# A two-layer hybrid encoder on one core: in the FFN's second product, low parts issued with their high parts and one of them moved to VectorE, and the last residual kept in quarters

## The chip, the cores and the metric

The kernel runs on 1 core of one Trainium2 chip. The metric is the time on the device of one execution, in microseconds; of three executions of the kernel before the median is 2655.85 us (2652.89 to 2661.12). Differences of about 0.3% (8 us) are what a measurement of this kernel can tell from none. All numbers of the trace come from one profiled execution, which took 2654.51 us.

## The reference

Two pre-norm residual layers on a sequence of 1024 tokens with 1024 channels, all in float32: a gated DeltaNet layer, then a chunked softmax attention layer, each followed by a gated feed-forward network with a short causal convolution, and a final RMSNorm.

```python
def conv_ffn(xn, w_up, conv_w, conv_b, w_down):
    h = causal_dwconv(xn @ w_up, conv_w) + conv_b
    gate, val = h[..., :FFN_DIM], h[..., FFN_DIM:]
    return (jax.nn.silu(gate) * val) @ w_down

def reference(x, ...):
    h = x
    for layer in range(2):
        h = h + (gated_deltanet(...) if layer == 0 else chunk_attention(...))
        h = h + conv_ffn(rmsnorm(h, f_norm[layer]), f_w_up[layer], f_conv[layer], f_conv_b[layer], f_w_down[layer])
    return rmsnorm(h, final_norm)
```

FFN_DIM is 2816, that is 22 blocks of 128 channels for the gate and 22 for the value.

## The kernel before, in words

**High and low parts.** A float32 operand of a matrix product is cut in two: a high part, a rounded copy that ScalarE (ACT) makes (`cut_high`, line 1378), and a low part, the difference of the operand and its high part (`cut_low`, through the helper of line 1357), which GpSimd (POOL) or VectorE (DVE) computes. `triple` (lines 1390 to 1392) then issues three matmuls for each product: high by high, low by high, high by low. TensorE (PE) so needs both parts, and a low part that is late stops it at the second or third matmul.

**The FFN.** Both layers call `ffn`. The first product (`w_up`) is made per block j of 128 channels, and both products are made by a scheme of seven block products in place of eight, with sums and differences of the operands made before and of the results after. A product of the first kind is `product(j, n)`: its operand `uh`, `ul` is cut from the weights `r` by `operand`, one step of VectorE where a difference is needed (`r<-r,r`), one of ScalarE, one of GpSimd. Results go to `keep`, `gpre` and `vpre` (`after`), then through the three taps of the convolution (`taps`: `val` and `gate`, lines 1473 and 1476), `silu` (line 1479) and `gated` (`val<-val,gate`).

The second product (`w_dn`) takes 18 of the 22 blocks in 9 groups g of two, again with seven block products n, in the order 1, 2, 5, 3, 6, 7, 4 (`ORDER`). One is `second(g, n)`, 12 matmuls into `pd`. Its two operands are `dh`, `dl`, cut from the weights `a` and their sum `ay` by `weights(g, n)`, and `eh`, `el`, cut from the hidden blocks `val` by `channels(g, n)`. `channels` makes the difference that some n need on VectorE (5, 6, 7 and 4), casts `eh` on ScalarE and returns the computation of `el` as a function that is called one step later: on GpSimd for n = 5, 6, 7, on VectorE for 1, 2, 3, 4. The results are copied by ScalarE or added by VectorE into `stage` (`drain`), and GpSimd's queue adds them into DRAM with accumulating DMAs (`send`, line 1711). The last 4 blocks (18 to 21) are multiplied plainly, with weights `fr` loaded by `load_last` and cut to `fh`, `fl` by `cut_last`.

**What sets the order.** The order is written out by hand. `step` appends a piece of work for TensorE to `seq`; `at(i, f, rank)` puts the work of the other engines ahead of step i, by rank within the step. At the end the lists are issued step by step; every engine then runs its own instructions strictly in that order, and waits for data by semaphores. A step of TensorE is 12 matmuls. A second product at step p has `channels` at p - 3 with rank 1.1, the low part at p - 2 with rank 1.1, `weights` at p - 3 with rank 1.2; `operand` has rank 1, `drain` 0, `send` 0.5, taps 2 and more, loads of weights 3. In the steady part a group takes 21 steps: 14 of the first product and 7 of the second, every third one. `eh`, `el`, `dh` and `dl` have two buffers each, `uh` and `ul` three.

**The end of the second layer.** `fin_at` is the step of the last second product, `end` that of the last first product. The residual of the second layer lies in DRAM in `d_r1`, 8 tiles of 128 x 1024 (`quarter` picks 512 columns of one), and `load_r(t)` brings the 128 tokens of tile t from it: for each of two halves c two DMAs of 128 x 2 x 128 each, on SyncE's (SP) queue. TensorE adds them by a transposing matmul (`pf<-ident,res`, line 1863). `load_last(q)` loads the eight pieces of the last weights, also on SP's queue, from `pos[FP - 1, 1]` on, the step of the first product of block 21; `cut_last(q)` follows at `last_at[q]`. SP's queue issues in order. With line numbers of the profile: `a` loads 1652, `d_e` 1715, `fr` 1755 and 1760, `ht` 1836, `res` 1849.

Of the kernel before, what the change touches and what calls it, by code (L numbers as in the profile page):

```python
# [9 lines left out]
F32 = mybir.dt.float32  # L10
# [6 lines left out]
P = 128  # L17
SEQ = 1024
# [4 lines left out]
FP = 22  # L23
# [5 lines left out]
def trunk_kernel(  # L29
# [15 lines left out]
    nc = tc.nc  # L45
# [5 lines left out]
    dram = ctx.enter_context(tc.tile_pool(name="dram", bufs=1, space=bass.MemoryType.DRAM))  # L51
# [72 lines left out]
    def hs(s):  # L124
        return slice(s * HALF, (s + 1) * HALF)
# [370 lines left out]

    ctx_h = ExitStack()

    d_r0, d_r1 = [{(c, s, u): dram.tile([P, SEQ], F32, name=f"d_r{i}_{c}{s}{u}") for c in range(2) for s in range(2) for u in range(2)} for i in range(2)]
    quarter = lambda d, m, s: d[m // 4, s, m % 4 // 2][:, hs(m % 2)]  # L500
    d_y = [[dram.tile([P, HALF], F32, name=f"d_y{k}_{s}") for s in range(2)] for k in range(KT)]
    d_z = [[dram.tile([P, HALF], F32, name=f"d_z{k}_{s}") for s in range(2)] for k in range(KT)]
    d_v = [[dram.tile([P, HALF], F32, name=f"d_v{k}_{s}") for s in range(2)] for k in range(KT)]
# [1 line left out]
    with ExitStack() as ph:  # L505
# [140 lines left out]
        def heads(t):  # L646

            return t // 2, range(4 * (t % 2), 4 * (t % 2) + 4)
# [651 lines left out]
        with tc.manual_schedule(engines={mybir.EngineType.PE, mybir.EngineType.DVE, mybir.EngineType.Activation}):  # L1300
            tails = []
            acts, normed = [[[[None, None] for _ in range(KT)] for _ in range(2)] for _ in range(2)]
            for t in range(4):
                s, hds = heads(t)
# [47 lines left out]
    def ffn(layer, h, hp, xs, tail, d_r, last):  # L1352
# [3 lines left out]
        sub, add = ALU.subtract, ALU.add  # L1356
        tt = lambda eng, o, a, b, op: eng.tensor_tensor(o, a, b, op=op)  # L1357

        d_c = d_r if layer == 0 else {x_: dram.tile([P, SEQ], F32, name=f"d_c{x_[0]}{x_[1]}{x_[2]}") for x_ in d_r}
        d_e = [dram.tile([P, SEQ], F32, name=f"d_e{layer}_{u}") for u in range(2)]  # L1360
        left, right = ExitStack(), ExitStack()
        tp = left.enter_context(tc.tile_pool(name=f"ft{layer}", bufs=1, **SB))
# [9 lines left out]
        def at(i, f, rank=1):  # L1372

            jobs.setdefault(max(i, 0), []).append((rank, f))

        def cut_high(src, ring, copy=nc.scalar.copy):
            hi, lo = [(wd if ring == "e" else wf).tile([P, HALF], F32R, name=ring + x, tag=ring + x, bufs=RINGS[ring]) for x in "hl"]
            copy(hi, src)  # L1378
            return hi, lo

        def cut_low(src, hi, lo, eng):
            tt(eng, lo, src, hi.bitcast(F32), sub)

        def cut(src, ring, copy=nc.scalar.copy):
            hi, lo = cut_high(src, ring, copy)
            cut_low(src, hi, lo, nc.gpsimd)
            return hi, lo
# [6 lines left out]
        kc = [slice(k * P, (k + 1) * P) for k in range(4)]  # L1394
# [129 lines left out]
        pos = {}  # L1524
# [42 lines left out]
        end, fin_at = pos[FP - 1, 7], pos["d", NG - 1, 4]  # L1567
        early = pos["p", 1, 3]
        for i, (j, n) in due.items():
            if i < early:  # L1570
                low = []
# [76 lines left out]
        araw, aops, bops, banks, stage = {}, {}, {}, {}, {}  # L1648

        def load_a(g, q):  # L1650
            araw[g, q] = wd.tile([P, HALF], F32, name=f"a{q}", tag=f"a{q}", bufs=1)
            nc.sync.dma_start(out=araw[g, q], in_=w_dn[(2 * g + q % 10 - 1) * P : (2 * g + q % 10) * P, hs(q // 10 - 1)])

        def weights(g, n):
            a = lambda q: araw[g, q]
            if n == 5:
                araw[g, 0] = wd.tile([P, HALF], F32, name="ay", tag="ay", bufs=1)
                tt(nc.vector, a(0), a(21), a(22), add)
            elif n == 3:
                tt(nc.vector, a(0), a(0), a(11), sub)  # L1660
                tt(nc.vector, a(12), a(12), a(0), sub)
            elif n == 7:
                tt(nc.vector, a(21), a(11), a(21), sub)
            aops[g, n] = cut(a({1: 11, 2: 12, 5: 0, 3: 12, 6: 0, 7: 21, 4: 22}[n]), "d")

        def channels(g, n):
            b11, b12, b21, b22 = [conv_t[2 * g + k, 1][:, hs(s)] for k in range(2) for s in range(2)]
            if n == 5:
                tt(nc.vector, b11, b12, b11, sub)
            elif n == 6:  # L1670
                tt(nc.vector, b11, b22, b11, sub)
            elif n == 7:
                tt(nc.vector, b12, b22, b12, sub)
            elif n == 4:
                tt(nc.vector, b21, b21, b11, sub)
            src = {1: b11, 2: b21, 5: b11, 3: b22, 6: b11, 7: b12, 4: b21}[n]
            bops[g, n] = cut_high(src, "e")
            return lambda: cut_low(src, *bops[g, n], nc.gpsimd if n in (5, 6, 7) else nc.vector)

        def second(g, n):  # L1680
            new = n in (1, 5, 6)
# [38 lines left out]
        for g in range(NG):  # L1720
            p_ = {n: pos["d", g, n] for n in ORDER}
            b_ = {n: pos["d", g - 1, n] for n in ORDER} if g else {1: p_[1] - 4, 3: p_[1] - 4, 7: p_[1] - 4, 4: p_[1] - 3}
            for q, n in ((11, 7), (12, 3), (21, 7), (22, 4)):
                at(b_[n] - 2, lambda g=g, q=q: load_a(g, q), 3 + q / 100)
            for n in ORDER:
                at(p_[n] - 3, lambda g=g, n=n: weights(g, n), 1.2)
                low = []
                at(p_[n] - 3, lambda g=g, n=n, low=low: low.append(channels(g, n)), 1.1)
                at(p_[n] - 2, lambda low=low: low[0](), 1.1)
                at(p_[n] + 1, lambda g=g, n=n: drain(g, n), 0)  # L1730
                if n not in (3, 5):
                    at(p_[n] + 2, lambda g=g, n=n: send(g, n), 0.5)
# [17 lines left out]
        def load_last(q):  # L1750
            tag = ("a11", "a12", "r11", "r21", "r22", "r11", "r22", "r21")[q]
            wp_, bufs = (wd, 1) if tag[0] == "a" else (wf, 2)
            if layer == 0:
                t_ = wp_.tile([P, 4, P], F32, name="fr", tag=tag, bufs=bufs)
                nc.sync.dma_start(out=t_, in_=w_dn[k0 * P :, q * P : (q + 1) * P].rearrange("(k p) m -> p k m", p=P))
                t_ = t_.rearrange("p k m -> p (k m)")
            else:
                k, c = q // 2, q % 2
                t_ = wp_.tile([P, HALF], F32, name="fr", tag=tag, bufs=bufs)
                nc.sync.dma_start(out=t_, in_=w_dn[(k0 + k) * P : (k0 + k + 1) * P, hs(c)])  # L1760
            fw[q] = t_
# [7 lines left out]

        for q in range(8):  # L1770
            s = (1, 1, 2, 3, 4, 4, 5, 6)[q]
            at(pos[FP - 1, s], lambda q=q: load_last(q), 1)
            at(last_at[q], lambda q=q: cut_last(q), 1.5)

        if layer == 0:
# [55 lines left out]
        else:  # L1831
# [8 lines left out]
            def load_r(t):  # L1840

                for c in range(2):
                    if t < 4:
                        tag = ("eh", "el", "dh", "dl")[t % 2 * 2 + c]
                        r_ = (wd if tag[0] == "e" else wf).tile([P, 4, P], F32, name="res", tag=tag, bufs=2)
                    else:
                        r_ = actp.tile([P, 4, P], F32, name="res", tag=f"x{'hl'[c]}{t}_1")
                    for u in range(2):
                        nc.sync.dma_start(out=r_[:, 2 * u : 2 * u + 2], in_=d_r[c, t // 4, u].rearrange("p (f t) -> p f t", f=2)[:, :, kc[t % 4]])
                    res[t, c] = r_  # L1850

            def tile_of(t, ks):
# [358 lines left out]
    def norm_out(t, ht, fin):  # L2211
# [26 lines left out]
        return go()  # L2238

    ctx_f, _ = ffn(1, h, hp, normed, tails[0], d_r1, norm_out)  # L2240
    ctx_f.close()
    ctx_h.close()
# [56 lines left out]
```

## Time and profile before

| | |
|---|---|
| median of three executions | 2655.85 us (2652.89 to 2661.12) |
| the profiled execution | 2654.51 us |
| its span, first to last instruction | 2652.8 us, granted clock 0.994 |
| DVE, ACT, POOL busy | 1907.7, 1409.5, 1483.6 us |
| moved by DMA | 326.72 MB |
| steady second products of layer 0 and 1 | from about 755 to 1283 us and 2029 to 2554 us |
| last blocks and closing of layer 1 | from about 2554 us on |

A row of the timeline has the start, the duration (of several merged instructions, with their count behind the x), the engine, the source line, the operation, the tiles written and read, their shapes, and in brackets how long the engine was idle before and what ended that. L1357 and L1378 are lines of helpers that many operations share; the tiles tell them apart. `PEld` is the weight load of TensorE, which runs beside the matmuls.

### The profile page before, as it was taken

To read this page: it belongs to the slowest core of one execution; us is meant where nothing else is said; L and a number is where in the kernel's file an instruction comes from. 1 tells how busy PE (TensorE), PEld (TensorE's weight loads), DVE (VectorE), ACT (ScalarE), POOL (GpSimd) and SP (SyncE) were. 2 spreads that over 40 slices of the span, in tenths; PEclk is the share of its full clock that TensorE was granted. 3 is DMA by queue.
4 is the path that set the end of the run, shared out by engine and by line. 5 is a ranking of instruction groups with operands and counts; after the bars stand their busy time and mean duration, and the time that the engine had idled before them with its cause. 6 is when DMAs were issued, how large, how long until landed. Compare 5 with 4: busy or idle time off the path is not lost. (4 is left out here: it accounts for less than half of the span.)

```text
span 2652.8 us, 39417 instructions
## 1 busy us (share of the span) xinstructions
PE 2533.4 (95%) x13933; PEld 2067.2 (78%) x13933; DVE 1907.7 (72%) x3084; ACT 1409.5 (53%) x2714; POOL 1483.6 (56%) x1490
## 2 busy tenths in 40 slices
PE   7999899999999999999999999998999999999988
PEld 5878788888777777777778888887777777777767
DVE  5755764553788888888775666666478888888876
ACT  5444456564455555555455555555345555555543
POOL 3655544346367777777645444443344677777760
PEclk9999999999999999999999999999999999999999
DMA  4534435555337777667731111114232577776785
GB/s 127 139 99 119 121 105 156 157 163 165 88 89 154 146 149 143 136 142 155 195 113 48 51 51 48 43 48 141 91 93 84 142 140 147 146 149 139 150 183 175
DMA packets 317846, 326.72 MB, mean 123 GB/s; under 512 B 33232, under 2 KB 240848, under 8 KB 317648
## 3 DMA queue, kind: packets, MB, share of 16 engines
q1 hardware_dynamic: 286192, 219.07, 28.2%
q0 software_dynamic: 26560, 96.48, 20.9%
q10 hardware_dynamic: 4896, 8.65, 0.9%
q8 instruction: 110, 1.80, 0.3%
q14 instruction: 88, 0.72, 0.1%
HBM read 180.94 MB, written 143.20 MB: 122 GB/s over the span
## 5 line engine op out<-in xcount | busy, mean ns | idle before, releaser
L1357 POOL TENSOR_TENSOR ul<-r,uh 128x512 fp32r<-128x512 f32 x282 | 442.9, 1579 | 360.9 <-ACT uh L1378 348.1
L120 PE MATMUL acc<-xh,whi 128*128 128x512 f32 x896 | 375.1, 419 | 0.2 <-ACT xh L1096 0.2
L1378 ACT CAST uh<-r 128x512 fp32r<-128x512 f32 x296 | 180.0, 621 | 365.7 <-DVE r L1357 308.6
L121 PE MATMUL acc<-xl,whi 128*128 128x512 f32 x896 | 353.6, 395 | 1.6 <-POOL xl L379 1.0
L122 PE MATMUL acc<-xh,wlo 128*128 128x512 f32 x896 | 353.1, 394 | 0.5 <-POOL wlo L105 0.5
L105 POOL TENSOR_TENSOR wlo<-wraw,whi 128x256 fp32r<-128x256 f32 (+1 forms) x293 | 235.8, 834 | 199.9 <-ACT whi L103 160.1
L1392 PE MATMUL pu<-xh,ul 128*128 128x512 f32 x552 | 217.8, 395 | 17.3 <-POOL ul L1357 17.3
L1357 DVE TENSOR_TENSOR r<-r,r 128x512 f32<-128x512 f32 x168 | 211.7, 1260 | 19.1 <-POOL ul L1357 19.0
L1390 PE MATMUL pu<-xh,uh 128*128 128x512 f32 x552 | 215.8, 391 | 3.0 <-ACT uh L1378 1.6
L1391 PE MATMUL pu<-xl,uh 128*128 128x512 f32 x552 | 215.3, 390 | 1.0 <-POOL xl L379 1.0
L122 PEld LDWEIGHTS acc<-xh,wlo 128*128 128x128 f32 x896 | 168.8, 188 | 38.3 <-POOL wlo L105 1.0
L1476 DVE SCALAR_TENSOR_TENSOR val<-vpre,colt,val 128x1023 f32<-128x1023 f32 (+2 forms) x92 | 163.9, 1782 | 38.9 <-ACT val L1473 38.7
L121 PEld LDWEIGHTS acc<-xl,whi 128*128 128x128 f32 x896 | 170.2, 190 | 25.8 <-POOL xl L379 3.1
L120 PEld LDWEIGHTS acc<-xh,whi 128*128 128x128 f32 x896 | 169.9, 190 | 23.0 <-ACT xh L1096 1.0
L1696 ACT COPY stage<-pd 128x1024 f32<-128x1024 f32 x180 | 173.1, 1012 | 0.4 <-DMA d_r<-stage 0.4
L2029 POOL TENSOR_SCALAR sS<-sS,st 128x640 f32<-128x640 f32 (+4 forms) x128 | 88.1, 691 | 143.2 <-DVE st L2028 123.2
L1357 POOL TENSOR_TENSOR dl<-a,dh 128x512 fp32r<-128x512 f32 x90 | 144.2, 1602 | 28.9 <-ACT dh L1378 28.9
L1476 DVE SCALAR_TENSOR_TENSOR gate<-gpre,colt,gate 128x1023 f32<-128x1023 f32 (+2 forms) x92 | 150.6, 1637 | 0.2
L1392 PEld LDWEIGHTS pu<-xh,ul 128*128 128x128 f32 x552 | 103.6, 188 | 48.9 <-POOL ul L1357 27.9
L2027 ACT ACTIVATE sS<-sS,st 128x640 f32<-128x640 f32 (+4 forms) x128 | 89.2, 697 | 82.3 <-DVE st L2026 81.3
L1357 DVE TENSOR_TENSOR el<-val,eh 128x512 fp32r<-128x512 f32 x72 | 102.0, 1417 | 36.2 <-ACT eh L1378 35.9
L1390 PEld LDWEIGHTS pu<-xh,uh 128*128 128x128 f32 x552 | 103.7, 188 | 24.8 <-ACT uh L1378 2.0
(389 smaller groups left out, 7122.2 us busy)
## 6 DMA issues: line engine op xcount, KB each, us to landing
r<-in_f_w_up_dram SPq DMA_DIRECT2D x168, 256.0 KB, 4.2
d_r<-stage POOLq DMA_DIRECT2D x78, 512.0 KB, 7.6
d_c<-stage POOLq DMA_DIRECT2D x70, 512.0 KB, 7.7
a<-in_f_w_down_dram SPq DMA_DIRECT2D x72, 256.0 KB, 2.7
wraw<-in_a_w_in_dram SPq DMA_DIRECT2D x32, 512.0 KB, 4.7
d_e<-stage POOLq DMA_DIRECT2D x32, 512.0 KB, 8.9
wraw<-in_a_w_out_dram SPq DMA_DIRECT2D x16, 512.0 KB, 4.1
d_r<-h ACTq DMA_DIRECT2D x32, 256.0 KB, 3.9
```

Of the source, the lines that this page charges most:

```text
L105: nc.gpsimd.tensor_tensor(lo[:, c], raw[:, c], hi[:, c].bitcast(F32), op=ALU.subtract)
L120: mm(ps, hi[:, kw, wcol : wcol + P], rh[k][s], start=st, stop=False)
L121: mm(ps, hi[:, kw, wcol : wcol + P], rl[k][s], start=False, stop=False)
L122: mm(ps, lo[:, kw, wcol : wcol + P], rh[k][s], start=False, stop=sp)
L1357: tt = lambda eng, o, a, b, op: eng.tensor_tensor(o, a, b, op=op)
L1378: copy(hi, src)
L1390: mm(ps, w[0][:, cw], x[0], start=first, stop=False, skip_group_check=True)
L1391: mm(ps, w[0][:, cw], x[1], start=False, stop=False, skip_group_check=True)
L1392: mm(ps, w[1][:, cw], x[0], start=False, stop=last, skip_group_check=True)
L1476: nc.vector.scalar_tensor_tensor(t_[:, a:c1], p_[:, a - step : c1 - step], w[:, 2 - step : 3 - step], t_[:, a:c1], op0=ALU.mult, op1=ALU.add)
L1696: nc.scalar.copy(t_, ps)
L2027: nc.scalar.activation(S, S, AF.Exp, bias=st[:, 1:2], accum_out=st[:, 2:3])
```

## The change

It has four parts, all in `ffn`, but for the tile of DRAM.

1. The low part `el` of a second product is issued in the same step as its high part (p - 3), right behind it, no longer one step later. `weights` (rank 1.2) now comes ahead of `channels` (rank 1.4), so that ScalarE casts `dh` before `eh`; for n = 3 alone `eh` is cast first, and `el` computed between the two differences of the weights and the cast of `dh`.
2. The low part of n = 5 is computed by VectorE; GpSimd keeps 6 and 7.
3. The first two loads of the last weights go out at `fin_at + 1`, in place of `pos[FP - 1, 1]`.
4. `d_r1` is 4 tiles of 128 x 2048 (quarters) in place of 8 of 128 x 1024, and `load_r` loads each half of a tile with one DMA of 128 x 4 x 128 in place of two of half the size.

```diff
-    d_r0, d_r1 = [{(c, s, u): dram.tile([P, SEQ], F32, name=f"d_r{i}_{c}{s}{u}") for c in range(2) for s in range(2) for u in range(2)} for i in range(2)]
-    quarter = lambda d, m, s: d[m // 4, s, m % 4 // 2][:, hs(m % 2)]
+    d_r0 = {(c, s, u): dram.tile([P, SEQ], F32, name=f"d_r0{c}{s}{u}") for c in range(2) for s in range(2) for u in range(2)}
+    d_r1 = {(c, s): dram.tile([P, 2 * SEQ], F32, name=f"d_r1{c}{s}") for c in range(2) for s in range(2)}
+    quarter = lambda d, m, s: d[m // 4, s, m % 4 // 2][:, hs(m % 2)] if (0, 0, 0) in d else d[m // 4, s][:, hs(m % 4)]
...
-        def weights(g, n):
+        def weights(g, n, other=lambda: None):
...
             elif n == 3:
                 tt(nc.vector, a(0), a(0), a(11), sub)
                 tt(nc.vector, a(12), a(12), a(0), sub)
+                other()
...
             bops[g, n] = cut_high(src, "e")
-            return lambda: cut_low(src, *bops[g, n], nc.gpsimd if n in (5, 6, 7) else nc.vector)
+            if n != 3:
+                cut_low(src, *bops[g, n], nc.gpsimd if n in (6, 7) else nc.vector)
+            return lambda: cut_low(src, *bops[g, n], nc.vector)
...
             for n in ORDER:
-                at(p_[n] - 3, lambda g=g, n=n: weights(g, n), 1.2)
-                low = []
-                at(p_[n] - 3, lambda g=g, n=n, low=low: low.append(channels(g, n)), 1.1)
-                at(p_[n] - 2, lambda low=low: low[0](), 1.1)
+                if n == 3:
+
+                    def third(g=g):
+                        low = channels(g, 3)
+                        weights(g, 3, low)
+
+                    at(p_[n] - 3, third, 1.2)
+                else:
+                    at(p_[n] - 3, lambda g=g, n=n: weights(g, n), 1.2)
+                    at(p_[n] - 3, lambda g=g, n=n: channels(g, n), 1.4)
...
-            at(pos[FP - 1, s], lambda q=q: load_last(q), 1)
+            at(fin_at + 1 if q < 2 else pos[FP - 1, s], lambda q=q: load_last(q), 1)
...
-                    for u in range(2):
-                        nc.sync.dma_start(out=r_[:, 2 * u : 2 * u + 2], in_=d_r[c, t // 4, u].rearrange("p (f t) -> p f t", f=2)[:, :, kc[t % 4]])
+                    nc.sync.dma_start(out=r_, in_=d_r[c, t // 4].rearrange("p (f t) -> p f t", f=4)[:, :, kc[t % 4]])
```

More of the change, by code (lines that the diff above doesn't have):

```diff
@@ L1357, in ffn @@
         tt = lambda eng, o, a, b, op: eng.tensor_tensor(o, a, b, op=op)
-        d_c = d_r if layer == 0 else {x_: dram.tile([P, SEQ], F32, name=f"d_c{x_[0]}{x_[1]}{x_[2]}") for x_ in d_r}
+        d_c = d_r if layer == 0 else {(c, s, u): dram.tile([P, SEQ], F32, name=f"d_c{c}{s}{u}") for c in range(2) for s in range(2) for u in range(2)}
         d_e = [dram.tile([P, SEQ], F32, name=f"d_e{layer}_{u}") for u in range(2)]
```

## The prediction

> **What bounds the kernel now.** I read the page's head first, then the windows, then who TensorE (PE) waited for, then the timeline of one group. Engine shares and one window of the steady second products of layer 1:
>
> ```profile
> span 2652.8 us, 39417 instructions
> PE 2533.4 (95%) x13933; PEld 2067.2 (78%) x13933; DVE 1907.7 (72%) x3084; ACT 1409.5 (53%) x2714; POOL 1483.6 (56%) x1490
> 2220.00:2320.00 100.00, 97.95 (x423) 78.39 (x422) 85.12 (x75) 55.59 (x81) 73.52 (x57) 1.00 0.68 138
> ```
>
> PE bounds the kernel; the change leaves it the same instructions in the same order, so only its gaps can change. Matmuls follow each other 0.227 us apart, so the 423 of this window need about 96 us: some 4 in 100 are lost. Its waits (us in total, times, longest) in the second products, two rows of layer 1 and one of layer 0, then one of the end of layer 1:
>
> ```profile
> PE pu L1392 <- POOL ul L1357: 7.4, 15, 0.7
> PE pd L1392 <- POOL el L1357: 4.6, 9, 1.1
> PE pd L1391 <- POOL el L1357: 6.7, 10, 1.2
> PE pu L1390 <- ACT uh L1378: 5.8, 3, 3.6
> ```
>
> So two things are late: `el`, once a group, and `ul`, more often; at the end of layer 1 it is `uh`. Groups repeat every 59.9 us; in the one from 925.6 us on, the three late products are:
>
> ```profile
> 941.95 0.39 PE L1390 MATMUL pd<-eh,dh 128*128 128x512 f32 x1
> 942.95 0.50 PE L1391 MATMUL pd<-el,dh 128*128 128x512 f32 x1 [0.61 <-POOL el L1357]
> ...
> 954.37 0.39 PE L1391 MATMUL pu<-xl,uh 128*128 128x512 f32 x1
> 955.39 0.50 PE L1392 MATMUL pu<-xh,ul 128*128 128x512 f32 x1 [0.63 <-POOL ul L1357]
> ...
> 979.87 0.39 PE L1391 MATMUL pu<-xt1l,uh 128*128 128x512 f32 x1
> 980.37 0.50 PE L1392 MATMUL pu<-xt1h,ul 128*128 128x512 f32 x1
> ```
>
> Start to start, less 0.23 us for a matmul: n = 5 loses 0.77 us to `el`, the product on `xh` 0.79 and that on `xt1` 0.27 to `ul`.
>
> **Part by part: the low part of n = 5.** What held it up (the first row, DVE's wait for PE at the head of the stretch, is used further below):
>
> ```profile
> 931.27 0.69 DVE L1357 TENSOR_TENSOR vpre<-pu,keep 128x512 f32<-128x512 f32 x1 [1.12 <-PE pu L1392]
> ...
> 937.75 2.31 DVE L1476 SCALAR_TENSOR_TENSOR val<-vpre,colt,val 128x1022 f32<-128x1022 f32 x1
> 939.98 1.78 DVE L1357 TENSOR_TENSOR r<-r,r 128x512 f32<-128x512 f32 x1
> 941.68 2.30 DVE L1476 SCALAR_TENSOR_TENSOR gate<-gpre,colt,gate 128x1023 f32<-128x1023 f32 x1
> 943.90 2.58 DVE L1357 TENSOR_TENSOR r<-r,r 128x512 f32<-128x512 f32 x1
> ...
> 937.48 1.49 POOL L1357 TENSOR_TENSOR ul<-r,uh 128x512 fp32r<-128x512 f32 x1 [3.15 <-ACT uh L1378]
> 938.94 2.27 POOL L1357 TENSOR_TENSOR dl<-ay,dh 128x512 fp32r<-128x512 f32 x1
> 941.17 1.73 POOL L1357 TENSOR_TENSOR el<-val,eh 128x512 fp32r<-128x512 f32 x1
> 942.84 1.76 POOL L1711 DMA_DIRECT2D d_r<-stage  x2
> 944.00 1.93 POOL L1357 TENSOR_TENSOR ul<-r,uh 128x512 fp32r<-128x512 f32 x1
> ```
>
> The durations tell of turns. `r<-r,r` takes 0.68 us when POOL is quiet (977.27, quoted below) and 2.58 here, until just after POOL's `ul` has ended (945.93); `ul` takes 1.30 alone (973.04, below). From 937.48 to 946.48 the two engines pass the right to work back and forth: ul, val, dl, r, el, gate, ul, r. With `el` on DVE, ahead of the tap, the turns are ul, el, dl, val, r, gate, ul, r; by the unhindered durations, less the 0.04 to 0.08 by which neighbours overlap, they last 1.26 + 0.60 + 1.26 + 1.20 + 0.60 + 1.20 + 1.26 + 0.60 = 8.0 us in place of 9.0. `el` is then done some 1.5 us before PE needs it: the 0.77 us go. But the last `r` is what the late product on `xh` hangs on (its `ul` comes after `r`, a tap, `silu`, `uh`), and it gains only what the whole stretch gains, at most 1.0, less any delay of its start.
>
> The Trainium skill, "SBUF — State Buffer", section "SBUF: two separate sides", calls the port pair of VectorE and GpSimd an exclusive lock: an instruction of VectorE with two SBUF inputs and one of GpSimd block each other for their whole length. By that rule a move from GpSimd to VectorE frees only the difference of two durations, 18 times 1.30 - 0.68 = 11 us at most, and not the engine's 1.73; the trace agrees, by the 2.58 beside 0.68. Were the engines independent, the gain would be the whole stall, as in the first rival below.
>
> **The low part of n = 4, where the change adds a wait.**
>
> ```profile
> 972.22 0.68 DVE L1357 TENSOR_TENSOR val<-val 128x512 f32<-128x512 f32 x1
> 972.83 2.35 DVE L1357 TENSOR_TENSOR stage<-pd,stage 128x1024 f32<-128x1024 f32 x2
> 975.09 1.07 DVE L1357 TENSOR_TENSOR el<-val,eh 128x512 fp32r<-128x512 f32 x1
> 976.08 1.27 DVE L1476 SCALAR_TENSOR_TENSOR gate<-gpre,colt,gate 128x1023 f32<-128x1023 f32 x1
> 977.27 0.68 DVE L1357 TENSOR_TENSOR r<-r,r 128x512 f32<-128x512 f32 x1
> ...
> 972.94 0.62 ACT L1378 CAST eh<-val 128x512 fp32r<-128x512 f32 x1
> ...
> 973.04 1.30 POOL L1357 TENSOR_TENSOR ul<-r,uh 128x512 fp32r<-128x512 f32 x1 [1.46 <-ACT uh L1378]
> ...
> 978.75 1.57 POOL L1357 TENSOR_TENSOR ul<-r,uh 128x512 fp32r<-128x512 f32 x1 [1.45 <-ACT uh L1378]
> ```
>
> Today two `stage` adds lie between `val<-val` and `el`, and cover the cast. In the new order `el` stands ahead of them, and `eh` is cast after `dh`, one cast later (0.62 less the overlap): it ends near 974.1, POOL's `ul` holds DVE until 974.34, and DVE idles 1.4 us. Queued behind it: both adds, `gate`, and the `r` at 977.27, whose `ul` (978.75 to 980.32) is the one that PE waits for on `xt1`. Since `el` then takes 0.60 and not 1.0, the cost is 1.0 us. Half comes back: for n = 7 `dh` is cast first too, so POOL begins its `dl` and `el` 0.6 us sooner and DVE's tap beside them ends sooner. I take +0.5 us on `xt1`, between 0 and 1.0. For n = 1 and 2 `el` stands where it stood on DVE, and only `eh` comes a cast later. POOL's order is the old one without n = 5; n = 6, 7 and 3 are not late by the rows.
>
> This half microsecond also delays the next stretch of turns, which starts when DVE has waited for PE (931.27 in this group): 0.5 us of PE, and by my estimate 0.4 more, since the later cast of `eh` for n = 2 holds up the `stage` copies behind it on ACT, the DMAs that POOL issues for them, and POOL's next `ul`. Of the 1.0 us that the stretch gains 0.1 remains. So one group: n = 5 loses 0.8 less, `xt1` 0.5 more, `xh` some 0.2 more: -0.15 us net, 18 groups **-2.7 us**. Bounds: the whole stall gone, -0.77 x 18 = -13.9; on the other side the second rival.
>
> **The first loads of the last weights.** At the end of layer 1:
>
> ```profile
> 2578.06 2.31 DVE L1476 SCALAR_TENSOR_TENSOR gate<-gpre,colt,gate 128x1023 f32<-128x1023 f32 x1
> ...
> 2572.53 1.27 POOL L1357 TENSOR_TENSOR ul<-r,uh 128x512 fp32r<-128x512 f32 x1 [3.66 <-ACT uh L1378]
> ...
> 2571.84 0.62 ACT L1378 CAST uh<-r 128x512 fp32r<-128x512 f32 x1 [1.78 <-DVE r L1357]
> 2576.80 0.62 ACT L1766 CAST fh<-fr 128x512 fp32r<-128x512 f32 x1 [4.34 <-DMA fr<-in_f_w_down_dram]
> 2584.85 0.60 ACT L1378 CAST uh<-r 128x512 fp32r<-128x512 f32 x1
> ...
> 2585.51 0.80 PE L1390 MATMUL pu<-xt4h,uh 128*128 128x512 f32 x1 [3.58 <-ACT uh L1378]
> ...
> 2560.64 3.43 SPq L1849 DMA_DIRECT2D res<-d_r  x4
> 2564.11 1.18 SPq L1760 DMA_DIRECT2D fr<-in_f_w_down_dram  x2
> 2565.39 8.09 SPq L1849 DMA_DIRECT2D res<-d_r  x4
> ```
>
> ACT, in order, waits 4.34 us for `fr`, issued at 2564 behind residual loads; behind that cast stand `uh`, then `silu` and the `uh` for `xt4`. In SP's new order the two loads stand ahead of every residual load, and their buffers are free once the weights of the last n = 7 are subtracted. ACT's 4.34 us go. What is late next is DVE, whose chain fl, gate, hidl, gate, silu, uh runs beside POOL's `ul` and `fl`: with the cast at 2572.46, `ul` holds DVE's `fl` until 2573.8, so that `gate` begins at 2574.4 and not at 2573.7 (2578.06 - 4.34); one more turn costs 0.1. The `uh` of 2584.85 comes at 2581.3, 3.6 us sooner, and the rest to the end follows it: **-3.6 us**. Bounds: 0, if another load is late in its place, and -5.8, all that PE's three waits on `uh` hold. In layer 0 no such wait stands in the rows: 0.
>
> **The residual in quarters.** 16 DMA issues fewer on SP, the same bytes in the same runs of 512 bytes. No wait of PE names `res`, and its loads lie under the first products; value 0. With that cover gone a block like the 8.09 us above would show.
>
> **Sum.** 2654.51 (span 2652.8 and 1.7 around it) - 2.7 - 3.6 = **2648.2 us**; the profiled execution lies 1.3 below the median shown, within its spread.
>
> **The rivals.**
> *The stall goes and stays gone.* DVE has idle time in each group (1.12 us before 931.27, for one) and takes the moves for nothing; the end gains 5.8: 2654.5 - 13.9 - 5.8 = 2634.8. For it speaks that POOL sheds 1.73 us a group; against it the turns, which leave `xh` late.
> *DVE's waits for `eh` reach PE.* The slower side: n = 4 idles DVE 1.4 us, n = 5 about 0.8 (its cast, 0.62, and the way there and back). If all of it comes through at `xt1` and `xh`, 18 x 2.2 = 39.6 us, against 13.9 + 3.6: 2676.6. It turns slower when over 0.97 of the 2.2 us arrive. For it: DVE is busy 85% and in order; against: its waits for PE, as at 931.27, absorb delays.
> *The end doesn't shorten*, since SP or the DMA engines, busy with accumulating stores then, keep a later `fr` late: only -2.7, 2651.8.
>
> **How the numbers follow.** Forecast 0.52, first rival 0.22, second 0.12, third 0.14. About 0.3% (8 us) is what a measurement here can tell from no change: faster is below 2646.5, slower above 2662.5. The forecast's spread of some 5 us puts 0.18 of its 0.52 under 2646.5; with the first rival 0.40 faster. Slower is the second rival, 0.11. Same 0.49. The range, 2634 to 2661, takes in the first rival's time and the mild half of the second's; about 0.18 is left out.
>
> **What would show it.** Right: no PE row `<-POOL el`, `pd` of n = 5 without a gap; the wait on `xt1` grown to about 0.8, that on `xh` still 0.6 to 1.0; an idle DVE of about 1.4 us before the `el` of n = 4; no ACT wait on `fr`, the last `xt4` some 3.6 us nearer to the last `xt1`. Wrong: `xh` no longer late (first rival); new PE waits on `dl`, `el` of DVE or on `xt1` above 1.3 (second); ACT waiting on another `fr` (third).

## The result and the profile after

The changed kernel takes 2644.8 us (median of six, 2642.17 to 2646.48) against 2656.83 us (six, 2652.89 to 2661.12) for the kernel before, run beside it: a ratio of 0.9952, 95% interval 0.9939 to 0.9964. That is 12 us faster, more than the 0.3% bound. The forecast of 2648.2 lies 3.4 us above the measured time, and the range holds it; but the likeliest class had been no change (0.49), and faster, which came, had 0.40.

The head of the page after, the window of steady second products of layer 1, and PE's waits in the second products of layers 0 and 1 and in the end of layer 1. Source lines have moved by 1 to 10 (L1357 is now L1358, L1392 is L1393).

```profile
span 2642.0 us, 39392 instructions
PE 2526.0 (96%) x13933; PEld 2069.7 (78%) x13933; DVE 1845.3 (70%) x3102; ACT 1409.1 (53%) x2714; POOL 1455.6 (55%) x1472
2220.00:2320.00 100.00, 97.62 (x427) 79.33 (x426) 78.47 (x77) 56.66 (x82) 73.45 (x57) 1.00 0.70 141
PE pu L1393 <- POOL ul L1358: 11.9, 19, 0.9
PE pu L1393 <- POOL ul L1358: 11.0, 18, 0.7
PE pu L1391 <- ACT uh L1379: 4.3, 3, 2.6
```

427 matmuls in place of 423 now start in the window. DVE's busy time there falls by 6.7 us although it was given work: its instructions overlap GpSimd's less. (Over whole steady groups, by the rows of the timeline, DVE is busy for 47.3 us in place of 51.1, and both engines have an instruction in flight for 25.8 us in place of 30.5, DMA issues not counted.) The waits on `el` (6.7 us in layer 0 and 4.6 in layer 1) are gone but for 0.7 and 0.5 us; those on `ul` have grown from 7.1 and 7.4 us.

The span is 10.8 us shorter. The table says where, from the starts of the matmuls (us). A first group runs from its n = 1 to the n = 1 of the next group, the other eight from there to the last matmul of the last n = 4, and the end from that matmul to the first `pf`.

| stretch | before | after | |
|---|---|---|---|
| layer 0, first group of second products | 51.1 | 54.1 | +3.0 |
| layer 0, the other eight groups | 473.7 | 466.2 | -7.5 |
| layer 1, first group | 49.9 | 53.1 | +3.2 |
| layer 1, the other eight groups | 473.4 | 466.4 | -7.0 |
| layer 1, the end | 42.3 | 39.5 | -2.8 |
| all the rest | 1562.4 | 1562.7 | +0.3 |

So the steady groups gained over five times what the sum gave them, the end 2.8 us of the 3.6 that it gave, and the first groups lost 6 us that the sum didn't have. (The rest is +0.3 only as a whole: up to the first group of layer 0 it is 2.6 us longer, in the end of layer 0 1.0 longer, and between the layers 3.3 shorter.) Now one steady group of after, the one from 930.03 us (n = 1 starts there; the next starts at 989.09, 59.06 us later; before, 925.63 to 985.49, 59.86 us). PE's rows at the three products that had been late:

```profile
946.35 0.39 PE L1391 MATMUL pd<-eh,dh 128*128 128x512 f32 x1
946.57 0.39 PE L1392 MATMUL pd<-el,dh 128*128 128x512 f32 x1
...
957.55 0.39 PE L1392 MATMUL pu<-xl,uh 128*128 128x512 f32 x1
958.62 0.50 PE L1393 MATMUL pu<-xh,ul 128*128 128x512 f32 x1 [0.68 <-POOL ul L1358]
...
983.03 0.39 PE L1392 MATMUL pu<-xt1l,uh 128*128 128x512 f32 x1
983.97 0.50 PE L1393 MATMUL pu<-xt1h,ul 128*128 128x512 f32 x1 [0.56 <-POOL ul L1358]
```

Start to start, less 0.23: n = 5 no longer waits, the first product on `xh` loses 0.84 us (before 0.79), the one on `xt1` 0.71 (before 0.27). DVE and POOL in the same group:

```profile
935.66 0.69 DVE L1358 TENSOR_TENSOR vpre<-pu,keep 128x512 f32<-128x512 f32 x1 [1.08 <-PE pu L1393]
942.95 1.02 DVE L1358 TENSOR_TENSOR el<-val,eh 128x512 fp32r<-128x512 f32 x1 [0.69 <-ACT eh L1379]
946.12 0.68 DVE L1358 TENSOR_TENSOR r<-r,r 128x512 f32<-128x512 f32 x1
946.72 1.27 DVE L1477 SCALAR_TENSOR_TENSOR gate<-gpre,colt,gate 128x1023 f32<-128x1023 f32 x1
947.92 1.78 DVE L1358 TENSOR_TENSOR r<-r,r 128x512 f32<-128x512 f32 x1
...
974.86 0.68 DVE L1358 TENSOR_TENSOR val<-val 128x512 f32<-128x512 f32 x1
976.67 0.84 DVE L1358 TENSOR_TENSOR el<-val,eh 128x512 fp32r<-128x512 f32 x1 [1.13 <-ACT eh L1379]
980.89 0.68 DVE L1358 TENSOR_TENSOR r<-r,r 128x512 f32<-128x512 f32 x1
...
945.06 1.77 POOL L1715 DMA_DIRECT2D d_r<-stage  x2
947.54 1.61 POOL L1358 TENSOR_TENSOR ul<-r,uh 128x512 fp32r<-128x512 f32 x1 [0.70 <-ACT uh L1379]
```

Two readings. From `vpre` to the end of the second `r` it is 14.04 us (935.66 to 949.70); before, 15.21 (931.27 to 946.48). An `r` of 1.78 has become one of 0.68, the `gate` of 2.30 one of 1.27 and the `r` of 2.58 one of 1.78, since POOL, with one instruction less, issues DMAs and waits for ACT just then. And at n = 4 DVE does wait for the cast, 1.13 us: from `val<-val` to `r` it is 6.03 us, before 5.05 (972.22 to 977.27).

The end of layer 1, after:

```profile
2528.45 0.98 SPq L1770 DMA_DIRECT2D fr<-in_f_w_down_dram  x2
...
2545.95 0.50 PE L1393 MATMUL pu<-xt1h,ul 128*128 128x512 f32 x1 [0.89 <-POOL ul L1358]
...
2565.36 0.61 ACT L1776 CAST fh<-fr 128x512 fp32r<-128x512 f32 x1
2565.51 0.50 PE L1391 MATMUL pu<-xt1h,uh 128*128 128x512 f32 x1 [0.67 <-ACT uh L1379]
...
2574.74 0.50 PE L1391 MATMUL pu<-xt4h,uh 128*128 128x512 f32 x1 [2.58 <-ACT uh L1379]
```

The cast of `fr` waits for nothing now. From the last `xt1` to the last `xt4` it is 9.23 us (2565.51 to 2574.74), before 13.00 (2572.51 to 2585.51). But the `xt1` behind the last second product waits 0.89 us, where before it was a quarter of that:

```profile
2553.00 0.50 PE L1392 MATMUL pu<-xt1h,ul 128*128 128x512 f32 x1 [0.21 <-POOL ul L1357]
```

### The profile page after: what moved, and what is told of

Its sections match the earlier page's. It is cut to its first block, busy times and chain, and to the rows that moved or that the text cites. A ratio compares the mean times of both kernels' runs of the same rounds, so it can differ in the third digit from the quotient of the medians.

```text
span 2642.0 us, 39392 instructions
## 1 busy us (share of the span) xinstructions
PE 2526.0 (96%) x13933; PEld 2069.7 (78%) x13933; DVE 1845.3 (70%) x3102; ACT 1409.1 (53%) x2714; POOL 1455.6 (55%) x1472
## 4 chain that ended last, share of the span: by engine, by line
PE 47%; POOL 13%; issue 12%; DVE 12%; ACT 4%; DMA 2%; POOLq 0%; SPq 0%; ACTq 0%; DVEq 0%
POOL ul L1358 5%; PE pu L1393 5%; PE acc L120 4%; PE acc L121 4%; PE acc L122 4%; PE pu L1391 4%; PE pu L1392 4%; POOL dl L1358 3%; DVE r L1358 2%; DVE val L1477 2%; PE acco L120 2%; PE acco L122 2%; PE acco L121 2%; PE ptp L2058 2%; PE pd L1393 1%
## 5 line engine op out<-in xcount | busy, mean ns | idle before, releaser
L1358 POOL TENSOR_TENSOR ul<-r,uh 128x512 fp32r<-128x512 f32 x282 | 434.7, 1550 | 380.8 <-ACT uh L1379 362.1
L1393 PE MATMUL pu<-xh,ul 128*128 128x512 f32 x552 | 218.0, 395 | 16.9 <-POOL ul L1358 16.8
L1392 PE MATMUL pu<-xl,uh 128*128 128x512 f32 x552 | 215.3, 390 | 1.0 <-POOL xl L379 1.0
L122 PEld LDWEIGHTS acc<-xh,wlo 128*128 128x128 f32 x896 | 169.5, 189 | 38.5 <-POOL wlo L105 1.0
L1358 DVE TENSOR_TENSOR r<-r,r 128x512 f32<-128x512 f32 x168 | 179.7, 1069 | 19.2 <-POOL ul L1358 19.2
L1477 DVE SCALAR_TENSOR_TENSOR val<-vpre,colt,val 128x1023 f32<-128x1023 f32 (+2 forms) x92 | 154.9, 1683 | 38.5 <-ACT val L1474 38.4
L1358 DVE TENSOR_TENSOR el<-val,eh 128x512 fp32r<-128x512 f32 x90 | 99.0, 1100 | 90.8 <-ACT eh L1379 90.8
L1358 POOL TENSOR_TENSOR dl<-a,dh 128x512 fp32r<-128x512 f32 x90 | 151.9, 1688 | 18.0 <-ACT dh L1379 18.0
L1393 PEld LDWEIGHTS pu<-xh,ul 128*128 128x128 f32 x552 | 103.6, 188 | 48.6 <-POOL ul L1358 27.8
L1477 DVE SCALAR_TENSOR_TENSOR gate<-gpre,colt,gate 128x1023 f32<-128x1023 f32 (+2 forms) x92 | 134.4, 1460 | 0.2
```

The source lines that it names most:

```text
L122: mm(ps, lo[:, kw, wcol : wcol + P], rh[k][s], start=False, stop=sp)
L1392: mm(ps, w[0][:, cw], x[1], start=False, stop=False, skip_group_check=True)
L1393: mm(ps, w[1][:, cw], x[0], start=False, stop=last, skip_group_check=True)
L1477: nc.vector.scalar_tensor_tensor(t_[:, a:c1], p_[:, a - step : c1 - step], w[:, 2 - step : 3 - step], t_[:, a:c1], op0=ALU.mult, op1=ALU.add)
```

## The experiments

The two traces gave an account (Theory 1 in the expectations) with four parts: n = 5 on VectorE is the whole gain of the groups; the new step costs time through n = 4; it costs more in the first group of each layer; the early loads shorten the end. Its rivals stand run by run in the expectations. Every run was measured beside the kernel before; ratios are to it, with 95% intervals, and compare runs better than the medians do (the kernel before had medians of 2654 to 2657 us beside them). The last four columns are from one profile of each run, in us, as in the table above, with layer 0 first; the group's length is from n = 1 to n = 1 of the group that starts nearest 925 us. In the runs that start from the changed kernel, `channels` again returns the computation of the low part, which the new order calls at once (`channels(g, n)()`); the diffs leave out lines that only repeat this.

| run | us | ratio | first groups | eight groups | end | group |
|---|---|---|---|---|---|---|
| before | 2656.83 | 1 | 51.1, 49.9 | 473.7, 473.4 | 42.3 | 59.86 |
| after | 2644.8 | 0.9952 (0.9939 to 0.9964) | 54.1, 53.1 | 466.2, 466.4 | 39.5 | 59.06 |
| n5_only | 2633.07 | 0.9918 (0.9907 to 0.9930) | 50.5, 50.0 | 463.7, 463.3 | 42.8 | 58.64 |
| step_only | 2665.56 | 1.0036 (1.0023 to 1.0049) | 54.9, 52.5 | 476.2, 476.4 | 40.4 | 60.26 |
| loads_only | 2648.15 | 0.9978 (0.9969 to 0.9987) | 50.5, 49.9 | 473.7, 473.3 | 40.5 | |
| quarters_only | 2654.86 | 1.0001 (0.9993 to 1.0010) | 51.0, 49.8 | 473.7, 473.3 | 43.7 | |
| four_late | 2627.25 | 0.9893 (0.9878 to 0.9908) | 52.4, 52.1 | 459.2, 459.3 | 41.2 | 58.03 |
| first_old | 2635.32 | 0.9927 (0.9914 to 0.9939) | 49.9, 49.3 | 466.4, 466.2 | 39.6 | |
| n5_loads | 2627.94 | 0.9903 (0.9889 to 0.9918) | 50.4, 49.5 | 463.7, 463.3 | 38.5 | |
| n5_loads_pool | 2625.85 | 0.9889 (0.9874 to 0.9904) | 50.4, 49.5 | 463.7, 463.3 | 36.4 | |
| first_four_old_pool | 2617.65 | 0.9861 (0.9842 to 0.9881) | 50.4, 48.8 | 459.4, 459.1 | 35.7 | |
| seven_new_pool | 2614.05 | 0.9851 (0.9834 to 0.9867) | 50.3, 49.7 | 458.7, 458.1 | 36.3 | 58.01 |

**n5_only**: the kernel before, with the low part of n = 5 on VectorE and nothing else.

```diff
-            return lambda: cut_low(src, *bops[g, n], nc.gpsimd if n in (5, 6, 7) else nc.vector)
+            return lambda: cut_low(src, *bops[g, n], nc.gpsimd if n in (6, 7) else nc.vector)
```

> The kernel before, with one edit: the low part of n = 5 is computed by VectorE, all else where it was (low parts one step after their high parts, loads and residual as before). Theory 1, the turns that VectorE and GpSimd take: the stall of n = 5 goes in every group, and since no low part waits right behind its cast, the wait on xt1 does not grow; a group takes 59.9 - 1.1 = about 58.8 us, the first groups keep their time, in all -18 to -22 us against the kernel before. Rival, the step is what counts: the low part of n = 5 is late because it is issued a step late, and on VectorE it is as late as on GpSimd; within 3 us of the kernel before.

Measured: 22 us faster than before, more than the whole change. The stretch of turns and the wait on `xh` in its group from 921.69 us:

```profile
927.33 0.69 DVE L1357 TENSOR_TENSOR vpre<-pu,keep 128x512 f32<-128x512 f32 x1 [1.08 <-PE pu L1392]
934.07 1.57 DVE L1357 TENSOR_TENSOR el<-val,eh 128x512 fp32r<-128x512 f32 x1
939.59 1.78 DVE L1357 TENSOR_TENSOR r<-r,r 128x512 f32<-128x512 f32 x1
...
950.28 0.50 PE L1392 MATMUL pu<-xh,ul 128*128 128x512 f32 x1 [0.64 <-POOL ul L1357]
```

The stretch is 14.04 us (927.33 to 941.37), to the hundredth that of after, though here `el` doesn't wait for its cast. So the 0.69 us that DVE waits in after at n = 5 cost nothing, and the shorter stretch is the engine's doing, not the step's. A group is 1.22 us shorter than before.

**step_only**: the changed kernel, with the low part of n = 5 back on GpSimd, still in the step of its high part.

```diff
-            if n != 3:
-                cut_low(src, *bops[g, n], nc.gpsimd if n in (6, 7) else nc.vector)
-            return lambda: cut_low(src, *bops[g, n], nc.vector)
+            return lambda: cut_low(src, *bops[g, n], nc.gpsimd if n in (5, 6, 7) else nc.vector)
...
-                    at(p_[n] - 3, lambda g=g, n=n: channels(g, n), 1.4)
+                    at(p_[n] - 3, lambda g=g, n=n: channels(g, n)(), 1.4)
```

> The changed kernel without the moves of loads and engine: low parts in one step with their high parts, n = 5 still on GpSimd; the two early loads and the residual in quarters are kept. Theory 1: GpSimd's order is that of before, so n = 5 stays late by 0.8 us; n = 4 makes VectorE wait and xt1 loses 0.5 us more a group, the first group of each layer 3 us; against the kernel before +9 + 6 - 3 for the end, about +12 us, and +23 against the changed kernel. Rival, the step is what counts: n = 5 is no longer late, and the time is that of the changed kernel within 4 us (-8 to -14 against before).

Measured: 0.36% slower than before, in spite of the early loads. All three products that were late before are late (start to start, less 0.23, they lose 0.82, 0.78 and 0.67 us):

```profile
947.68 0.50 PE L1392 MATMUL pd<-el,dh 128*128 128x512 f32 x1 [0.66 <-POOL el L1358]
...
960.14 0.50 PE L1393 MATMUL pu<-xh,ul 128*128 128x512 f32 x1 [0.62 <-POOL ul L1358]
...
985.45 0.50 PE L1393 MATMUL pu<-xt1h,ul 128*128 128x512 f32 x1 [0.51 <-POOL ul L1358]
```

Making `el` a step sooner doesn't make it earlier while GpSimd computes it: the turns, not the place in the list, set when it is done. The step alone costs 0.40 us a group, and 2.6 to 3.8 in each first group.

**loads_only** and **quarters_only**: the kernel before with part 3 alone, and with part 4 alone (its lines of the diff above). The edit of loads_only:

```diff
-            at(pos[FP - 1, s], lambda q=q: load_last(q), 1)
+            at(fin_at + 1 if q < 2 else pos[FP - 1, s], lambda q=q: load_last(q), 1)
```

> The kernel before with the first two loads of the last weights at fin_at + 1, nothing else. Theory 1: the wait of ScalarE for them at the end of layer 1 goes, from the last second product to the first pf 42.2 us become 39.5, in all -2.7 us, groups unchanged. Rival, the residual's halved loads shorten the end: within 1 us of the kernel before, ScalarE still waits for fr.

> The kernel before with the residual of layer 1 in quarters and half as many loads of it, nothing else. Theory 1: worth nothing, within 1.5 us of the kernel before, the wait of ScalarE for fr stays near 4.3 us. Rival: SyncE's queue is what made fr late, and half as many issues ahead of it bring it 2 to 4 us sooner; -2 to -3 us.

Measured: the loads gain 1.8 us in the end of layer 1 and some 6 us by the medians; of the profile's 5.2 us 3.4 lie outside that stretch, most of them between the first `pf` of layer 0 and the first second product of layer 1 (713.7 us before, 711.1 here), a way that differs by 1.9 us between n5_loads and n5_loads_pool too (711.1 and 713.0), whose programs part only after it. So they are not shown to come from the loads. The quarters are worth nothing (0.9993 to 1.0010), and ScalarE still waits 4.76 us for `fr` with them.

**four_late**: the changed kernel, n = 4 alone scheduled as before.

```diff
+                if n == 4:
+                    at(p_[n] - 3, lambda g=g, n=n: weights(g, n), 1.2)
+                    low = []
+                    at(p_[n] - 3, lambda g=g, n=n, low=low: low.append(channels(g, n)), 1.1)
+                    at(p_[n] - 2, lambda low=low: low[0](), 1.1)
-                if n == 3:
+                elif n == 3:
```

> The changed kernel, but for n = 4 alone its second product is scheduled as before: high part first, low part one step later, behind the two stage adds. Theory 1: VectorE's idle 1.1 us ahead of the low part of n = 4 is what makes the wait on xt1 grow from 0.27 to 0.72; it goes back to 0.27, a group takes 58.65 us in place of 59.05, in all -7 us against the changed kernel, its first groups 1 us shorter each at most. Rival, the cast of the weights ahead of that of the hidden blocks is the cost, for all n: a group stays at 59.05 us, within 2 us of the changed kernel.

Measured: by the ratios 0.6% less than after, 16 us. The group falls from 59.06 to 58.03, and only one wait of PE is left in it, at `xh`:

```profile
953.97 0.50 PE L1393 MATMUL pu<-xh,ul 128*128 128x512 f32 x1 [0.58 <-POOL ul L1358]
```

So n = 4's wait is the cost of the new step, 1.0 us in every steady group. And four_late is 0.6 us a group shorter than n5_only, where Theory 1 expected no difference (58.65): the new order of the others gains something. Which of them, the last run shows.

**first_old**: the changed kernel, with the first group of each layer scheduled as before (n = 5 on GpSimd in it too).

```diff
-            if n != 3:
-                cut_low(src, *bops[g, n], nc.gpsimd if n in (6, 7) else nc.vector)
-            return lambda: cut_low(src, *bops[g, n], nc.vector)
+            return lambda: cut_low(src, *bops[g, n], nc.gpsimd if n in ((5, 6, 7) if g == 0 else (6, 7)) else nc.vector)
...
-                if n == 3:
+                if g == 0:
+                    at(p_[n] - 3, lambda g=g, n=n: weights(g, n), 1.2)
+                    low = []
+                    at(p_[n] - 3, lambda g=g, n=n, low=low: low.append(channels(g, n)), 1.1)
+                    at(p_[n] - 2, lambda low=low: low[0](), 1.1)
+                elif n == 3:
```

> The changed kernel, with the first group of each layer scheduled as in the kernel before (low parts a step later, n = 5 on GpSimd). Theory 1: the first groups lost 3.1 us each by the waits for high parts, since their block products stand closer together there; they go back to 51 and 50 us, the steady groups stay at 59.05; about -6 us against the changed kernel. Rival: the first groups are longer because the steps ahead of them run differently, or as a price of the steady order that is only paid there; within 2 us of the changed kernel.

Measured: by the ratios 0.25% less than after, 7 us; in the profile 4.2 and 3.8 us, in the first groups alone. What the new step does there, in after's first group of layer 0:

```profile
800.46 2.48 DVE L1358 TENSOR_TENSOR el<-val,eh 128x512 fp32r<-128x512 f32 x1 [1.18 <-ACT eh L1379]
802.86 2.34 DVE L1358 TENSOR_TENSOR stage<-pd,stage 128x1024 f32<-128x1024 f32 x2
804.21 0.47 PE L1391 MATMUL pd<-eh,dh 128*128 128x512 f32 x1 [0.46 <-DVE stage L1358]
805.12 1.27 DVE L1477 SCALAR_TENSOR_TENSOR gate<-gpre,colt,gate 128x1022 f32<-128x1022 f32 x1
806.48 1.06 ACT L1480 ACTIVATE gate<-gate 128x1024 f32<-128x1024 f32 x1 [6.06 <-DVE gate L1477]
808.10 0.50 PE L1391 MATMUL pu<-xh,uh 128*128 128x512 f32 x1 [0.89 <-ACT uh L1379]
```

DVE waits 1.18 us for `eh`; the adds to `stage` behind `el` are late for PE (0.46 us), and so is the `gate` behind them, `silu` behind that on ACT, and the `uh` behind `silu` (0.89 us). It is the queue that the prediction named for n = 4, and these two waits lose 1.65 us from start to start. They are not all: in the same group after also loses 0.80 us at `xt2` (761.84), 0.83 to `uh` and 0.84 to `ul` at `xt4` (776.25 and 777.66), and saves the 1.40 that before lost to the `el` of n = 5 (770.39).

**n5_loads**: n5_only with the early loads. **n5_loads_pool**: with the low parts of pieces 0 and 2 of layer 1's last weights on GpSimd too, that is with the `fl` of VectorE's last chain moved.

```diff
-            cut_low(fw[q], hi, lo, nc.gpsimd if q % 2 else nc.vector)
+            cut_low(fw[q], hi, lo, nc.gpsimd if q % 2 or layer == 1 and q < 3 else nc.vector)
```

> The kernel before with two edits: the low part of n = 5 on VectorE, and the first two loads of the last weights at fin_at + 1. Theory 1: the two are worth the same together as alone, 58.65 us a group and an end (last second product to first pf) of 38.5 to 40 us; -24 to -27 us against the kernel before, about 2629. Rival: the loads gain only where the stage before is late; no more than the -21 of the first edit alone.

> As n5_loads, and in layer 1 the low parts of pieces 0 and 2 of the last weights are computed by GpSimd, no longer by VectorE. Theory 1: after the loads are on time the end hangs on VectorE's chain fl, gate, hidl, gate, silu, uh; without the fl in it the late uh comes 1.4 to 2.5 us sooner, and a second fl gone gives up to 1 us more; 2 to 3.5 us below n5_loads. Rival: GpSimd, which has the ul products in the same stretch, becomes late in its place; within 1 us of n5_loads or slower.

Measured: beside n5_only the loads shorten the end by 4.3 us (42.8 to 38.5; alone it was 1.8), and the whole by 0.15%, 4 us, with intervals that overlap a little. The two runs with the loads part ahead of the late `xt4`, where loads_only waits 0.70 us at an `xt2` and n5_loads doesn't; why is not shown. `fl` off VectorE takes another 2.1 us off the end (38.5 to 36.4), but here too the intervals of the two ratios overlap. With the step of before and the two useful parts of the change, n5_loads is by the ratios 13 us faster than after.

**first_four_old_pool**: the changed kernel with first group and n = 4 as before (n = 5 of the first group on GpSimd), and the pieces on GpSimd. **seven_new_pool**: n5_loads_pool with quarters, and n = 7 alone, in all groups but the first, in the new order.

```diff
-                if n == 3:
+                if g == 0 or n != 7:
+                    at(p_[n] - 3, lambda g=g, n=n: weights(g, n), 1.2)
+                    low = []
+                    at(p_[n] - 3, lambda g=g, n=n, low=low: low.append(channels(g, n)), 1.1)
+                    at(p_[n] - 2, lambda low=low: low[0](), 1.1)
+                elif n == 3:
```

> The changed kernel, with the first group of each layer and n = 4 of every group scheduled as before, and the low parts of pieces 0 and 2 of layer 1's last weights on GpSimd. Theory 1: the parts add up: 58.05 us a group as with n = 4 late, first groups of 50 and 49.3 us, an end of about 36.5 us: 2 + 2 + 3 us below the kernel with n = 4 late alone, about 2620. Rival: what the first groups win is lost in the second one, whose work starts later; no better than the kernel with n = 4 late, 2627.

> n5_loads_pool with one edit more (and the residual in quarters): n = 7 of all groups but the first casts the weights ahead of the hidden block, its low part in the same step. Theory 1: this alone is what the new order gives a group, as VectorE's tap beside GpSimd's el of n = 7 ends 0.6 us sooner: the wait on xt1 (0.28) goes, 58.05 to 58.2 us a group, 16 x 0.5 = 8 us less than n5_loads_pool, about 2618. Rival: the gain of the new order comes from n = 1, 2, 5 and 6; a group stays at 58.65 us, within 2 us of n5_loads_pool.

Measured: in first_four_old_pool the parts add up as expected, by the ratios 24 us under the changed kernel and 8 under four_late. That speaks against the rival, no gain over four_late: the two intervals just overlap, but the first groups are 2.0 and 3.3 us shorter. seven_new_pool has the lowest median, 2614.05 us, 1.5% under the kernel before and by the ratios 27 us under the changed one; its interval overlaps that of first_four_old_pool. Its eight groups take 5.0 and 5.2 us less than those of n5_loads_pool, which is all that the new order gained in four_late (4.5 and 4.0 less than n5_only): n = 7 alone brings it. First n5_only, then seven_new_pool, from `vpre` to the `r` on which `xt1` hangs:

```profile
955.59 0.69 DVE L1357 TENSOR_TENSOR vpre<-pu,keep 128x512 f32<-128x512 f32 x1 [3.12 <-PE pu L1392]
959.28 1.30 POOL L1357 TENSOR_TENSOR dl<-a,dh 128x512 fp32r<-128x512 f32 x1 [1.89 <-ACT dh L1378]
960.73 2.17 DVE L1476 SCALAR_TENSOR_TENSOR val<-vpre,colt,val 128x1023 f32<-128x1023 f32 x1
972.13 0.68 DVE L1357 TENSOR_TENSOR r<-r,r 128x512 f32<-128x512 f32 x1
```

```profile
952.39 0.69 DVE L1358 TENSOR_TENSOR vpre<-pu,keep 128x512 f32<-128x512 f32 x1 [3.13 <-PE pu L1393]
955.46 1.31 POOL L1358 TENSOR_TENSOR dl<-a,dh 128x512 fp32r<-128x512 f32 x1 [1.28 <-ACT dh L1379]
957.52 1.58 DVE L1477 SCALAR_TENSOR_TENSOR val<-vpre,colt,val 128x1023 f32<-128x1023 f32 x1
968.33 0.68 DVE L1358 TENSOR_TENSOR r<-r,r 128x512 f32<-128x512 f32 x1
```

With `dh` cast first, GpSimd's `dl` begins 3.07 us after `vpre` in place of 3.69, DVE's tap is held up less (1.58 for 2.17) and ends 0.60 us sooner, and `r` starts 15.94 us after `vpre` in place of 16.54.

## Why the prediction came out as it did

- **The stall of n = 5 goes**: right, and its price was too low. The prediction gave the stretch of turns 8.0 us in place of 9.0; it shrank by 1.17 (from the `ul` on, from 9.00 to 7.77), and n5_only's group by 1.22. The bound that it worked out from the Trainium skill, "SBUF — State Buffer", section "SBUF: two separate sides" (the difference of two durations, 11 us over 18 groups at most), fell: n5_only gained 20 us in its sixteen later groups alone (473.7 - 463.7 and 473.4 - 463.3). The page's rule itself, mutual blocking, still agrees with the rows; what the bound left out is that the shorter row of turns puts an `r` and a `gate` beside GpSimd's DMA issues and its wait for ACT (946.12 to 947.99 in after), where they take their short durations.
- **n = 4 waits for its cast**: right in mechanism and size. Idle 1.13 us (1.4 foreseen), path 0.98 longer (1.0 foreseen), 1.0 us of the group (four_late). Half comes back by n = 7: right, 0.6 us by seven_new_pool. Net 0.40 us a group (n5_only against after 0.42, before against step_only 0.40), against the +0.5 taken; the start-to-start loss at `xt1` grew by 0.44.
- **The failed step** is the sentence "Of the 1.0 us that the stretch gains 0.1 remains", with the 0.4 us put on the later cast of `eh` for n = 2. From `vpre` (935.66) to the late `ul` product (958.62) after takes 22.96 us, before 24.12 (931.27 to 955.39), so 1.16 less; the remainder of the group grows from 35.74 to 36.10, so 0.36 more, no more than the wait on `xt1` grew. Nothing is left for the 0.4. The sum of the group is 1.16 - 0.36 = 0.80 us, not 0.15 (the prediction's three items, 0.8, 0.5 and 0.2, come to 0.1). Of the 0.7 between 0.1 and 0.8, 0.4 is this term, 0.16 the stretch and 0.14 `xt1`. The estimate of 0.4 came from no row; it was a chain of three queues (ACT, POOL's issue, POOL's next `ul`), and it breaks at the first. ACT casts `eh` and `dh` of n = 2 one behind the other (928.14 and 928.66 before; swapped, `dh` 932.57 and `eh` 933.09, after), and the `stage` copies stand behind both in either order, so a later `eh` makes them no later. Before, then after:

```profile
929.18 1.92 ACT L1696 COPY stage<-pd 128x1024 f32<-128x1024 f32 x2
...
932.40 1.93 POOL L1357 TENSOR_TENSOR ul<-r,uh 128x512 fp32r<-128x512 f32 x1
```

```profile
933.61 1.92 ACT L1700 COPY stage<-pd 128x1024 f32<-128x1024 f32 x2
...
936.84 1.94 POOL L1358 TENSOR_TENSOR ul<-r,uh 128x512 fp32r<-128x512 f32 x1
```

Against `vpre` (931.27 and 935.66), the copies start 2.09 us ahead before and 2.05 after, and POOL's `ul` 1.13 and 1.18 us behind it: 0.05 us in place of 0.4.

- **All 18 groups alike**: wrong, and unseen. The prediction read one steady group and multiplied by 18; the first group of each layer has its own spacing and lost 3.0 and 3.2 us. Sixteen groups gave -14.5 us, where 16 x 0.15 = 2.4 was forecast, and two gave +6.2, where 0.3 was to be gained: errors of -12.1 and +6.5 us, so this one hid over half of the other.
- **The first loads of the last weights**: right. ACT's wait is gone, `fl`, `gate`, `hidl`, `gate`, `silu`, `uh` is the chain that is late next (2566.01 to 2574.68 in after), and `xt4` came 3.8 us nearer to `xt1` (3.6 foreseen). One us of it is lost before, 0.7 at the `xt1` behind the last n = 4 (0.89 in place of 0.21), so the end as a whole shortened by 2.8. That term wasn't carried over from the part on n = 4 to the end.
- **The residual in quarters**: 0, right.
- **The rivals**: the stall neither stayed gone as if DVE had room (`xh` still loses 0.84), nor did DVE's waits for `eh` reach PE in the whole of their 2.2 us (that of n = 5 was swallowed, that of n = 4 came through). The end did shorten. The first rival's 13.9 us for the groups was by chance nearest to the sixteen steady ones, for another reason.

The measured time lies near the forecast partly by luck: of the error of -12.1 us in the steady groups, +6.5 in the first groups, +0.8 in the end and +0.3 in the rest leave only -4.5.

What stays open: the stretches outside the groups differ between runs with the same instructions there. The way to the first group of layer 0 takes 755.2 us in before and 758.9 in quarters_only, and 752.5 to 758.9 over the twelve profiles. The granted clock differs there as well (from 300 to 400 us it is 1.00 in before and 0.97 in quarters_only; of 23 executions of before, the fastest, 2650.41 us, had 0.993 over the whole and the slowest, 2660.64, had 0.989), but no run shows how much of it that makes. And the waits of the first groups were removed together, not one by one.

## What to carry to other kernels

When two engines block each other, price a moved instruction by writing out the new order of turns against everything that the other engine does, its DMA issues and idle time too, and not by the difference of two durations. Before putting a consumer right behind its producer on another engine, look at what lies in between: work that hides the producer's latency is free, and what is queued behind the consumer pays when it goes; so change the order item by item, since here n = 4 lost 1.0 us and n = 7 won 0.6 by the same edit. And a repeating group's price holds for the steady ones only: look at the first and the last for themselves.

## What the runs showed of the hardware

**A wait costs PE more than its length.** The matmul behind a late one, in after the one behind 958.62, starts 0.33 us after it, not 0.23:

```profile
958.95 0.40 PE L1391 MATMUL pu<-xh,uh 128*128 128x512 f32 x1
```

So each short stall of the groups shown costs some 0.1 us on top, and the late matmul itself lasts 0.50 in place of 0.39.

**The granted clock fell at a wait in some runs, and not in others.** Windows of 5 us (the third number from the end is the clock) of before, then after, then first_old, each around the late `xt4`:

```profile
2585.00:2590.00 5.00, 4.37 (x9) 2.98 (x10) 3.80 (x5) 1.20 (x3) 1.27 (x1) 0.50 0.17 52
```

```profile
2575.00:2580.00 5.00, 3.38 (x13) 2.13 (x13) 3.68 (x4) 1.20 (x3) 1.34 (x2) 1.00 0.20 70
```

```profile
2570.00:2575.00 5.00, 5.00 (x17) 3.88 (x16) 2.79 (x3) 3.61 (x6) 2.75 (x3) 0.68 0.60 165
```

Before waited 3.58 us for that `xt4`, after 2.58 and first_old 2.54 (its `xt4` is at 2566.82); so the length of the wait alone doesn't decide. Nor does it take a long one: in n5_loads_pool the clock fell behind waits of 1.03 and 0.89 us at `xt1`, and in seven_new_pool the same two waits left it at 1.00. n5_loads_pool, then seven_new_pool:

```profile
2550.00:2555.00 5.00, 3.88 (x10) 2.82 (x11) 2.95 (x3) 2.68 (x5) 4.75 (x3) 0.72 1.09 271
```

```profile
2535.00:2540.00 5.00, 3.07 (x13) 1.91 (x12) 2.94 (x4) 3.13 (x5) 3.38 (x3) 1.00 1.07 244
```

By windows of 0.5 us the clock is at 0.50 for 3.4 us in n5_loads_pool and for 6.8 in before and first_old. The Trainium skill, "TensorE: Matmul & The Clock Gate", section "Part 1: The HAM clock gate (the "warmup" mystery)", has a window of activity of about 3.4 us that runs freely, so that it depends on the phase what a gap does; that agrees with these lengths and with the difference between runs that have the same waits, though not with gaps shorter than the window being enough.

What a fall costs depends on what PE would have done. From the late `xt4` to the first `pf` it is 8.69 us in after, at full clock throughout, and 8.72 in before and 8.82 in first_old, where 5.4 and 6.4 us of that way run at 0.50: at full clock PE waits 0.62, 1.00 and 0.62 us for `ul`, `uh` and `ul` there (in after), and the slower matmuls only fill such waits. In four_late, whose clock fell behind those waits, it is 10.27 us, so its end is some 1.5 us longer by it.
